# The first layer's values computed with tokens on partitions: x stationary, 512 weight columns moving

## The chip, the cores and the metric

The kernel runs on one core of a Trainium2 chip, as one launch. The metric is the device time of that launch in microseconds. Engines are named as in the profile: PE is TensorE, DVE VectorE, ACT ScalarE, POOL GpSimd, SP the queue that issues all DMAs.

## What is computed

One inference step of a two-layer trunk on 320 tokens: 256 of a prompt and 8 x 8 of a sample. The width is 1024. Layer 0 mixes tokens by chunked spatial gating, layer 1 by an mLSTM; each is followed by a gated feed-forward part. The change touches layer 0 alone:

```python
h = rmsnorm(x, norm_mix_g)                # 320 x 1024
u, v = split(gelu(h @ w_in), 2)           # w_in: 1024 x 4096; u and v: 320 x 2048
v = (v - mean(v)) * rsqrt(var(v) + eps) * ln_g + ln_b    # over the 2048, per token
mixed = einsum('gts,bnsgd->bntgd', tril(w_s), chunks of v) + b_s
y = (u * mixed) @ w_out                   # 2048 x 1024
```

The sample's normalised v is an output too. All tensors are fp32 and the product has to keep more bits than one fp32r matmul keeps. So each operand is split into a high part (rounded to fp32r) and a low part (the rest), and a product is three matmuls: high x high, high x low, low x high.

## The kernel before

x is held transposed: xT has 128 partitions (a slice of the width), 8 such slices k, and 320 columns (tokens). norm_block (L158 to L164) multiplies a slice by the norm's gain and splits it into xh (ACT, L163) and xl (DVE, L164). The token's own factor of the RMS norm, rc, is applied later, behind the matmuls: as a scale per partition where tokens lie on partitions, or as the row rb where they lie along columns. It needs the sum of squares (square_block), then norm_cols (three small matmuls, ms on DVE, a power on POOL at L196), and norm_row for rb.

Weights come from DRAM as blocks of 128 output columns: a tile "raw" of 128 x 8 x 128. weights() (L57) writes out the whole order of use as a list. prefetch(n, m) (L101) issues the DMAs of the first n entries on SP (L109) and splits the first m into wh (ACT copy, L124) and wl (DVE subtraction, L125). take() calls it with four loads and one split ahead. The pool "raw" has four buffers, wh and wl have three each. chunk and block run the matmuls: for each k, wh and then wl are stationary (128 x 128) and x moves, 320 columns at a time: wh x xh, wh x xl, wl x xh, into one PSUM bank of tag "pm". mm (L44) pins the matmuls to the order of the program; the other engines' orders are set by a scheduler that goes by the order of the code, free buffers and issue_after.

layer_a first computes v, weight blocks 16 to 31. Block b gives 128 values for 320 tokens, transposed to what is wanted. So DVE copies it to SBUF (vT, L289), v_nat turns it with three PE transposes (L50) into PSUM tiles pvt with tokens on partitions, and after each fourth block ACT applies gelu with scale rc (L269) and DVE takes the statistics (L270). Between the blocks stand the squares (after block 1), norm_cols and load_ws (the masks and mixing matrices, after block 3), norm_row (after block 5) and row_sums (after block 10). The third token tile holds the last 128 tokens, of which the lower 64 partitions repeat prompt tokens. Then come the 16 blocks of u, the normalisation of v (v_stats, normalise), the mixing (mix), and the output product. PSUM has three banks of tag "pm" and five of tag "pa".

run() starts with ten warm-up matmuls on a tile of ones (pw), loads the first 16 columns of vecs (8 KB), and then four times: two slices of x in one DMA (320 KB), a weight piece, the split of both slices. The first weight block is cut in pieces of 2, 2 and 4 slices, the second in 4 and 4.

Of the kernel before, what the change touches and what calls it, by code (L numbers as in the profile page):

```python
# [22 lines left out]
KD = D // P  # L23
DA = 2048
KA = DA // P
NH = 8
# [11 lines left out]
class Net:  # L38
# [19 lines left out]
    def weights(self):  # L58

        I = self.I  # L60
        q = []

        def add(w, b, *groups, k0=0):
            for kn in groups:
                q.append((w, b, k0, kn))
                k0 += kn

        add(I["a_win"], 16, 2, 2, 4)
        add(I["a_win"], 17, 4, 4)
        for b in [*range(18, 32), *range(16)]:  # L70
            add(I["a_win"], b, 8)
        for b in range(KD):
            add(I["a_wo"], b, 8, 8)

        def ffn(l):
            for b in range(2 * KF):
                add(I["f_up"][l], b, 8)
            for b in range(KD):
                add(I["f_dn"][l], b, 8, 7, 7)

        ffn(0)
# [21 lines left out]
    def prefetch(self, n, m):  # L103

        nc = self.nc
        while len(self.loaded) < min(n, len(self.wq)):
            w, b, k0, kn = self.wq[len(self.loaded)]
            raw = self.wraw.tile([P, 8, P], F32, tag="raw", name="raw")
            nc.sync.dma_start(raw[:, :kn, :], w[b, :, k0:k0 + kn, :])  # L109
            self.loaded.append(raw)  # L110
        while len(self.halved) < min(m, len(self.wq)):
            i = len(self.halved)
            raw, kn = self.loaded[i], self.wq[i][3]
            self.loaded[i] = None
# [9 lines left out]
            self.last_split = nc.scalar.copy(wh[:, :kn, :], raw[:, :kn, :])  # L124
            nc.vector.tensor_tensor(wl[:, :kn, :], raw[:, :kn, :], wh[:, :kn, :].bitcast(F32), op=SUB)  # L125
            self.halved.append((wh, wl))

# [16 lines left out]
    def block(self, kt, rhs):  # L144

        ps = self.psm.tile([P, 512], F32, tag="pm", name="pm")
        done = 0
        while done < kt:
            kn = self.wq[self.used][3]
            self.chunk(ps, lambda k: rhs(done + k), done == 0, done + kn == kt)  # L150
            done += kn
        return ps


    def vec(self, c):
# [26 lines left out]
    def norm_cols(self, parts=None, twice=False):  # L182

        nc = self.nc
        parts = parts or [self.acc]
        pc = self.psa.tile([P, 512], F32, tag="pa", name="pc")
        pv = pc[:, 0:6].rearrange("p (t e) -> p t e", e=2)
        for t in range(3):
            for i, a in enumerate(parts):
                self.mm(pv[:, t, :], self.tokens(a, t), self.ones[:, :2], i == 0, i == len(parts) - 1)  # L190
        rc = self.tp.tile([P, 3], F32, tag="rc", name="rc", bufs=2)
        ms = self.tp.tile([P, 3], F32, tag="ms", name="ms", bufs=2)
        nc.vector.tensor_scalar(ms, pv[:, :, 0], 1.0 / D, EPS, op0=MULT, op1=ADD)
        if twice:
            nc.scalar.copy(ms[:64, 2:3], ms[64:, 2:3])
        nc.gpsimd.tensor_tensor(rc, ms, self.mhalf.to_broadcast([P, 3]), op=ALU.pow)  # L196
        self.rc = rc

    def norm_row(self):
# [28 lines left out]
    def layer_a(self):  # L228
        nc, tc, I, O = self.nc, self.tc, self.I, self.O
        with tc.tile_pool(name="ya", bufs=1) as yp, tc.tile_pool(name="la", bufs=1) as lp:  # L230
# [11 lines left out]
            pvt = {}  # L242

            def load_ws():
                nc.sync.dma_start(ws, I["a_ws"])
                nc.sync.dma_start(trit, I["trit"])
                nc.gpsimd.memset(wss[:64], 0.0)
# [3 lines left out]
                nc.gpsimd.tensor_tensor(ws, ws, trit.unsqueeze(1).to_broadcast([P, NH, P]), op=MULT)  # L251
                nc.gpsimd.tensor_tensor(wss[64:], wss[64:], bdt[64:].unsqueeze(1).to_broadcast([64, NH, 64]), op=MULT)

            def row_sums():
                for i in range(2):
# [1 line left out]
                    self.mm(pr, self.ones, ws[:, 4 * i:4 * i + 4, :], True, True)  # L257
                    nc.scalar.copy(rsum[:, 4 * i:4 * i + 4, :].rearrange("p g t -> p (g t)"), pr)

            def v_nat(b, vT):  # L260
                q, c = b // 4, b % 4
                if c == 0:
                    pvt[q] = [self.psa.tile([P, 512], F32, tag="pa", name="pvt") for _ in range(3)]
                for t in range(3):
                    self.tr(pvt[q][t][:, c * P:(c + 1) * P], self.tokens(vT, t), self.ident)
                if c == 3:
                    for t in range(3):
                        vv = v[:, t, q * 512:(q + 1) * 512]
                        nc.scalar.activation(vv, pvt[q][t], AF.Gelu_apprx_tanh, scale=self.rc[:, t:t + 1])  # L269
                        nc.vector.bn_stats(st[:, t, q, :], vv)  # L270

            prev = None
            for b in range(16):
                ps = self.block(KD, self.x_rhs)
                if b == 1:
                    with tc.issue_after(self.last_split.ins):
                        for m in range(KD):
                            self.square_block(m)
                if b == 3:
                    self.norm_cols()  # L280
                    load_ws()
                if b == 5:
                    self.norm_row()
                if b == 10:
                    row_sums()
                if prev is not None:
                    v_nat(b - 1, prev)
                prev = lp.tile([P, T], F32, tag="vT", name="vT", bufs=2)
                nc.vector.tensor_copy(prev, ps[:, :T])  # L289

            ve = lp.tile([P, 3], F32, name="ve_a")
            rs = lp.tile([P, 3], F32, name="rstd_a")

            def v_stats():
                for t in range(3):
                    nc.vector.bn_aggr(mv[:, t, :], st[:, t])
                nc.vector.tensor_scalar(ve, mv[:, :, 1], EPS, None, op0=ADD)
                nc.gpsimd.tensor_tensor(rs, ve, self.mhalf.to_broadcast([P, 3]), op=ALU.pow)
                nc.vector.scalar_tensor_tensor(ve, mv[:, :, 0], -1.0, rs, op0=MULT, op1=MULT)

            def normalise(q):
                for t in range(3):
                    vv = v[:, t, q * 512:(q + 1) * 512]
                    nc.scalar.activation(vv, vv, AF.Identity, scale=rs[:, t:t + 1], bias=ve[:, t:t + 1])

            def v_rows(q):
                cs = slice(q * 512, (q + 1) * 512)
# [30 lines left out]
            for b in range(16):  # L338
                ps = self.block(KD, self.x_rhs)
                if b == 0:  # L340
                    v_nat(15, prev)
# [582 lines left out]
    def run(self):  # L924
        nc, tc, I, O = self.nc, self.tc, self.I, self.O
        with tc.tile_pool(name="const", bufs=1) as cp, tc.tile_pool(name="xp", bufs=1) as xp, \
# [15 lines left out]
            nc.scalar.activation(warm, self.mhalf, AF.Gelu_apprx_tanh)  # L942
            nc.vector.memset(self.ones, 1.0)
            pw = psa.tile([P, 512], F32, tag="pa", name="pw")
            for i in range(10):
                self.mm(pw[:, :P], self.ones, self.ones, True, True)
            nc.sync.dma_start(self.vecs[:, :16], I["vecs"][:, :16])
            for i in range(4):
                nc.sync.dma_start(self.xT[:, 2 * i:2 * i + 2, :], I["xT"][:, 2 * i:2 * i + 2, :])
                self.prefetch(i + 1, 0)  # L950
                for m in (2 * i, 2 * i + 1):
                    self.norm_block(m, V_MIX)
                self.prefetch(i + 1, min(i + 1, 3))
            nc.sync.dma_start(self.ident, I["ident"])
            nc.sync.dma_start(self.vecs[:, 16:], I["vecs"][:, 16:])
            self.layer_a()
            self.ffn(0, V_MIX + 8)
            self.layer_b()
# [15 lines left out]
def _lay_out(i):  # L974
# [6 lines left out]
    a["a_win"] = _blocks(i["a_w_in"][0])  # L981
# [80 lines left out]
```

## Time and profile before

| | us |
|---|---|
| median of three runs | 983.28 (981.37 to 983.53) |
| the profiled execution, own time | 980.58 |
| its span, first to last instruction | 978.8 |
| PE busy | 965.3 |
| DVE busy | 700.0 |
| ACT busy | 511.4 |
| POOL busy | 95.7 |

The page of the profile gives busy time by engine, the chain of work that ended last, and the costliest groups of instructions. The trace behind it answers by window, in order of time, by tile and by shape. A matmul's record begins when it starts and overlaps the next, so the pace of a run of matmuls is read from the chain (time of a piece over its count), not from the mean of one. A plain fp32 matmul leaves two records. The granted clock was 0.997 over the span. A weight block's matmuls are named pm; pvt are the transposes of v, pc, pb and pr those of norm_cols, norm_row and row_sums.

### The profile page before, as it was taken

Reading aid. Unit: us, or ns where it says so; the run is one execution under the profiler, and the core shown is the slowest. Engines: PE = TensorE matmul, PEld = TensorE weight load, DVE = VectorE, ACT = ScalarE, POOL = GpSimd, SP = SyncE. Lnnn points to the kernel's source line nnn. Section 1 sums busy time; section 2 is a strip of 40 time slices with the busy share of each in tenths; the row PEclk is TensorE's granted clock in tenths of the full one; section 3 lists DMA queues with packets and bytes.
Section 4 is the critical chain, followed back from the end, with each engine's and each line's share of the span. In section 5 each row is a group of like instructions: output and inputs, shape, how many; then the busy total and the mean of one; then the engine's idle time right before and its main releaser. Section 6 shows DMA issues by size and latency. Waiting matters only on the chain.

```text
span 978.8 us, 17589 instructions
## 1 busy us (share of the span) xinstructions
PE 965.3 (99%) x6695; PEld 958.9 (98%) x6695; DVE 700.0 (72%) x1358; ACT 511.4 (52%) x918; POOL 95.7 (10%) x268
## 2 busy tenths in 40 slices
PE   8999999999999999999999999999999999999996
PEld 8999999999999999999999999999999999999996
DVE  6647985577777764559999988787787777775442
ACT  6437444455544543349676766565655455544332
POOL 0100000010000000013231111111101000000000
PEclk9999999999999999999999999999999999999998
DMA  8535334444444454554464654544354444444541
GB/s 280 201 130 157 128 136 149 151 150 152 151 142 156 141 158 141 155 172 166 170 210 169 205 192 163 175 168 143 127 204 148 151 151 151 152 146 148 145 131 54
DMA packets 55591, 154.63 MB, mean 158 GB/s; under 512 B 6563, under 2 KB 17443, under 8 KB 55507
## 3 DMA queue, kind: packets, MB, share of 16 engines
q1 hardware_dynamic: 55506, 153.51, 47.1%
q8 instruction: 53, 0.87, 0.4%
q14 instruction: 32, 0.25, 0.1%
HBM read 141.55 MB, written 11.94 MB: 157 GB/s over the span
## 4 chain that ended last, share of the span: by engine, by line
PE 82%; issue 10%; DVE 4%; ACT 2%; DMA 1%; SPq 0%; POOL 0%; DVEq 0%; POOLq 0%; ACTq 0%
PE pm L47 74%; PE num L47 2%; PE pcs L47 1%; PE pmix L47 1%; DVE wl L125 1%; DMA C<-in_C 1%; DVE bcv L599 1%; PE pvt L50 1%; ACT wh L124 0%; PE pv L50 0%; PE psc L47 0%; PE pCp L47 0%; DMA xT<-in_xT 0%; PE phn L50 0%; PE pg L47 0%
## 5 line engine op out<-in xcount | busy, mean ns | idle before, releaser
L124 ACT CAST wh<-raw 128x1024 fp32r<-128x1024 f32 (+3 forms) x253 | 257.7, 1019 | 354.4 <-PE pm L47 196.8
L47 PE MATMUL pm<-xh,wh 128*128 128x320 f32 x1344 | 419.3, 312 | 1.4 <-ACT wh L124 1.4
L47 PE MATMUL pm<-xh,wl 128*128 128x320 f32 x1344 | 415.9, 309 | 2.1 <-DVE wl L125 1.9
L47 PE MATMUL pm<-xl,wh 128*128 128x320 f32 x1344 | 415.1, 309 | 0.0
L125 DVE TENSOR_TENSOR wl<-raw,wh 128x1024 fp32r<-128x1024 f32 (+3 forms) x253 | 299.6, 1185 | 117.9 <-ACT wh L124 115.2
L47 PEld LDWEIGHTS pm<-xh,wl 128*128 128x128 f32 x1344 | 252.3, 188 | 3.4 <-DVE wl L125 3.4
L47 PEld LDWEIGHTS pm<-xh,wh 128*128 128x128 f32 x1344 | 252.5, 188 | 2.4 <-ACT wh L124 2.1
L47 PEld LDWEIGHTS pm<-xl,wh 128*128 128x128 f32 x1344 | 252.5, 188 | 0.2
L47 PE MATMUL pm<-yh_f,wh 128*128 128x320 f32 x352 | 109.0, 310 | 0.0
L47 PE MATMUL pm<-yl_f,wh 128*128 128x320 f32 x352 | 108.5, 308 | 0.0
L47 PE MATMUL pm<-yh_f,wl 128*128 128x320 f32 x352 | 108.5, 308 | 0.0
L47 PEld LDWEIGHTS pm<-yl_f,wh 128*128 128x128 f32 x352 | 66.1, 188 | 0.0
L47 PEld LDWEIGHTS pm<-yh_f,wh 128*128 128x128 f32 x352 | 66.1, 188 | 0.0
L47 PEld LDWEIGHTS pm<-yh_f,wl 128*128 128x128 f32 x352 | 66.1, 188 | 0.0
L393 DVE SCALAR_TENSOR_TENSOR fcv<-fpad,vecs,fcv 128x336 f32<-128x336 f32 x88 | 49.6, 566 | 2.2 <-ACT fcv L391 0.7
L216 DVE TENSOR_TENSOR xT<-pm,xT 128x320 f32<-128x320 f32 x40 | 19.5, 490 | 41.9 <-PE pm L47 41.9
L47 PE MATMUL pm<-ylb,wh 128*128 128x320 f32 x128 | 39.9, 312 | 0.5 <-DVE ylb L813 0.4
L47 PE MATMUL pm<-yhb,wh 128*128 128x320 f32 x128 | 40.0, 312 | 0.4 <-ACT yhb L812 0.4
L47 PE MATMUL pm<-yhb,wl 128*128 128x320 f32 x128 | 39.6, 309 | 0.0
L47 PE MATMUL pm<-yh_a,wh 128*128 128x320 f32 x128 | 39.6, 309 | 0.0
L47 PE MATMUL pm<-yh_a,wl 128*128 128x320 f32 x128 | 39.5, 308 | 0.0
L47 PE MATMUL pm<-yl_a,wh 128*128 128x320 f32 x128 | 39.5, 308 | 0.0
(254 smaller groups left out, 1261.0 us busy)
## 6 DMA issues: line engine op xcount, KB each, us to landing
raw<-in_f_up SPq DMA_DIRECT2D x88, 512.0 KB, 3.2
raw<-in_b_win SPq DMA_DIRECT2D x48, 512.0 KB, 3.4
raw<-in_a_win SPq DMA_DIRECT2D x30, 512.0 KB, 3.3
raw<-in_f_dn SPq DMA_DIRECT2D x32, 448.0 KB, 3.2
C<-in_C SPq DMA_DIRECT2D x32, 258.0 KB, 3.7
raw<-in_a_wo SPq DMA_DIRECT2D x16, 512.0 KB, 3.7
raw<-in_f_dn SPq DMA_DIRECT2D x16, 512.0 KB, 3.5
out_Cs<-C SPq DMA_DIRECT2D x32, 256.0 KB, 2.7
```

Of the source, the lines that this page charges most:

```text
L47: self.pin(self.nc.tensor.matmul(out, lhsT, rhs, start=start, stop=stop))
L50: self.pin(self.nc.tensor.transpose(out, in_, ident))
L124: self.last_split = nc.scalar.copy(wh[:, :kn, :], raw[:, :kn, :])
L125: nc.vector.tensor_tensor(wl[:, :kn, :], raw[:, :kn, :], wh[:, :kn, :].bitcast(F32), op=SUB)
L216: self.nc.vector.tensor_tensor(x, ps[:, :T], x, op=ADD)
L393: nc.vector.scalar_tensor_tensor(cv, pd[:, i:i + NC], self.vec(w + i * KF), cv, op0=MULT, op1=ADD)
L599: nc.vector.scalar_tensor_tensor(cv, pd[:, i:i + NC], self.vec(w + 16 * i), cv, op0=MULT, op1=ADD)
```

## The change

In the v half the operands change places. The weights of v are laid out anew as a_wv: four groups of 512 columns, and in a tile two slices k of 512 columns each. `natural` keeps x stationary and moves 512 weight columns:

```python
def natural(self, ps, xs, hooks):
    k = 0
    while k < KD:
        for f in hooks.get(k, ()):
            f()
        (wh, wl), kn = self.take()
        for j in range(0, kn, 4):
            w, u = [x[:, j:j + 4, :].rearrange("p a b -> p (a b)") for x in (wh, wl)]
            h0, h1 = self.xh[:, k, :P], self.xh[:, k, P:TP]
            l0, l1 = self.xl[:, k, :P], self.xl[:, k, P:TP]
            a, z = k == 0, k == KD - 1
            for t, x, y, st, sp in ((0, h0, w, a, False), (1, h1, w, a, False), (0, l0, w, False, False),
                                    (1, l1, w, False, False), (2, xs[:, k, :], w, a, False), (0, h0, u, False, z),
                                    (1, h1, u, False, z), (2, xs[:, k, :], u, False, z)):
                self.mm(ps[t], x, y, st, sp)
            k += 1
```

Each group fills three whole PSUM banks: two for the prompt's two tiles and one for the sample. xs holds in its columns 0 to 63 the sample's xh and in 64 to 127 its xl, both copied by POOL; so the third bank holds the two parts' products on separate halves of the partitions, and they are added afterwards. (That also adds xl x wl, which was left out before.) Groups 0 and 2 use the banks of tag "pm", 1 and 3 those of "pa".

```diff
-        add(I["a_win"], 16, 2, 2, 4)
-        add(I["a_win"], 17, 4, 4)
-        for b in [*range(18, 32), *range(16)]:
+        for b in range(4):
+            add(I["a_wv"], b, 4, 4)
+        for b in range(4, 16):
+            add(I["a_wv"], b, 8)
+        for b in range(16):
             add(I["a_win"], b, 8)
...
-            self.last_split = nc.scalar.copy(wh[:, :kn, :], raw[:, :kn, :])
+            if i:
+                self.last_split = nc.scalar.copy(wh[:, :kn, :], raw[:, :kn, :])
+            else:
+                nc.vector.tensor_copy(wh[:, :kn, :], raw[:, :kn, :])
...
+            def x_parts(k):
+                self.norm_block(k, V_MIX)
+                nc.gpsimd.tensor_copy(xs[:, k, :64], self.xh[:, k, TP:T])
+                nc.gpsimd.tensor_copy(xs[:, k, 64:], self.xl[:, k, TP:T])
+
+            for k in range(4):
+                x_in(k)
+                if k:
+                    self.prefetch(k + 1, 0)
+            x_parts(0)
+            nc.sync.dma_start(self.ident, I["ident"])
+            nc.sync.dma_start(self.vecs[:, 16:], I["vecs"][:, 16:])
+            nc.gpsimd.memset(mv, 0.0)
+            nc.gpsimd.memset(v[:64, 2, :], 0.0)
...
+                with tc.issue_after(self.rc_made.ins):
+                    nc.gpsimd.tensor_tensor(ws, ws, trit.unsqueeze(1).to_broadcast([P, NH, P]), op=MULT)
+                    nc.gpsimd.tensor_tensor(wss[64:], wss[64:], bdt[64:].unsqueeze(1).to_broadcast([64, NH, 64]), op=MULT)
...
-            def v_nat(b, vT):
...
-                ps = self.block(KD, self.x_rhs)
...
+            def group(q, hooks):
+                pool, tag = (self.psa, "pa") if q % 2 else (self.psm, "pm")
+                vps[q] = [pool.tile([P, 512], F32, tag=tag, name="pv_a") for _ in range(3)]
+                self.natural(vps[q], xs, hooks)
+
+            def v_out(q):
+                cs = slice(q * 512, (q + 1) * 512)
+                ps = vps.pop(q)
+                tmp = lp.tile([P, 512], F32, tag="vs", name="vs_a", bufs=2)
+                nc.scalar.copy(tmp[64:], ps[2][:64])
+                nc.vector.tensor_tensor(tmp[64:], ps[2][64:], tmp[64:], op=ADD)
+                for t, src, r in ((0, ps[0], slice(0, P)), (1, ps[1], slice(0, P)), (2, tmp, slice(64, P))):
+                    vv = v[r, t, cs]
+                    nc.scalar.activation(vv, src[r], AF.Gelu_apprx_tanh, scale=self.rc[r, t:t + 1])
+                    nc.vector.bn_stats(st[r, t, q, :], vv)
...
+            group(0, {k: (lambda k=k: rows_in(k),) for k in range(KD)})
+            group(1, {0: (squares,), 6: (self.norm_cols, lambda: v_out(0))})
+            group(2, {0: (lambda: v_out(1), load_ws), 4: (self.norm_row,)})
+            group(3, {0: (lambda: v_out(2),), 4: (row_sums,)})
+            v_out(3)
...
-            for i in range(10):
+            self.prefetch(1, 0)
+            for i in range(7):
                 self.mm(pw[:, :P], self.ones, self.ones, True, True)
-            nc.sync.dma_start(self.vecs[:, :16], I["vecs"][:, :16])
-            for i in range(4):
-                nc.sync.dma_start(self.xT[:, 2 * i:2 * i + 2, :], I["xT"][:, 2 * i:2 * i + 2, :])
-                self.prefetch(i + 1, 0)
-                for m in (2 * i, 2 * i + 1):
-                    self.norm_block(m, V_MIX)
-                self.prefetch(i + 1, min(i + 1, 3))
```

The slices of x now come one by one (160 KB each): SP issues weight piece 0, vecs, x row 0, x row 1, weight piece 1, x row 2, weight piece 2, and so on. Group 0 takes weight pieces of one slice k (256 KB); the other groups take two slices (512 KB). Its hook rows_in(k) loads slice k + 4 of x and splits slice k + 1. The wh copy of piece 0 moves from ACT to DVE. In the built program the order on PE is that of `natural`; on POOL the power for rc stands ahead of the two mask products; SP places the loads of the masks in group 2. Vectors over v's third tile (statistics, gelu, normalisation) work on its upper 64 partitions, and its lower half is zeroed. The u half and all that follows keep their instructions.

More of the change, by code (lines that the diff above doesn't have):

```diff
@@ L152, in block @@
         return ps
+    def natural(self, ps, xs, hooks):
[3 more added lines that the diff above has]
+                f()
+            (wh, wl), kn = self.take()
+            for j in range(0, kn, 4):
[8 more added lines that the diff above has]
+                k += 1
     def vec(self, c):
@@ L195, in norm_cols @@
             nc.scalar.copy(ms[:64, 2:3], ms[64:, 2:3])
-        nc.gpsimd.tensor_tensor(rc, ms, self.mhalf.to_broadcast([P, 3]), op=ALU.pow)
+        self.rc_made = nc.gpsimd.tensor_tensor(rc, ms, self.mhalf.to_broadcast([P, 3]), op=ALU.pow)
         self.rc = rc
@@ L241, in layer_a, with x_in @@
             bdt = lp.tile([P, 64], F32, name="bdt")
-            pvt = {}
+            xs = lp.tile([P, KD, P], F32R, name="xs_a")
+            nc.sync.dma_start(self.vecs[:, :16], I["vecs"][:, :16])
+            def x_in(k):
+                nc.sync.dma_start(self.xT[:, k, :], I["xT"][:, k, :])
+            def x_parts(k):
[11 more added lines that the diff above has]
+            nc.gpsimd.memset(v[:64, 2, :], 0.0)
             def load_ws():
@@ L250, in load_ws @@
                 nc.sync.dma_start(bs, I["a_bs"].to_broadcast([P, NH, P]))
-                nc.gpsimd.tensor_tensor(ws, ws, trit.unsqueeze(1).to_broadcast([P, NH, P]), op=MULT)
-                nc.gpsimd.tensor_tensor(wss[64:], wss[64:], bdt[64:].unsqueeze(1).to_broadcast([64, NH, 64]), op=MULT)
+                with tc.issue_after(self.rc_made.ins):
+                    nc.gpsimd.tensor_tensor(ws, ws, trit.unsqueeze(1).to_broadcast([P, NH, P]), op=MULT)
+                    nc.gpsimd.tensor_tensor(wss[64:], wss[64:], bdt[64:].unsqueeze(1).to_broadcast([64, NH, 64]), op=MULT)
             def row_sums():
@@ L258, in row_sums @@
                     nc.scalar.copy(rsum[:, 4 * i:4 * i + 4, :].rearrange("p g t -> p (g t)"), pr)
-            def v_nat(b, vT):
[L261 to L270, printed above, removed]
@@ L272, in layer_a @@
-            prev = None
-            for b in range(16):
-                ps = self.block(KD, self.x_rhs)
[L275 to L289, printed above, removed]
+            def group(q, hooks):
+                pool, tag = (self.psa, "pa") if q % 2 else (self.psm, "pm")
+                vps[q] = [pool.tile([P, 512], F32, tag=tag, name="pv_a") for _ in range(3)]
+                self.natural(vps[q], xs, hooks)
@@ new lines, in squares, with rows_in @@
+            def squares():
+                with tc.issue_after(self.last_split.ins):
+                    for m in range(KD):
+                        self.square_block(m)
+            def rows_in(k):
+                if k + 4 < KD:
+                    x_in(k + 4)
+                if k + 1 < KD:
+                    x_parts(k + 1)
+            vps = {}
+            group(0, {k: (lambda k=k: rows_in(k),) for k in range(KD)})
+            group(1, {0: (squares,), 6: (self.norm_cols, lambda: v_out(0))})
@@ L295, in v_stats @@
                 for t in range(3):
-                    nc.vector.bn_aggr(mv[:, t, :], st[:, t])
+                    r = slice(64 * (t // 2), P)
+                    nc.vector.bn_aggr(mv[r, t, :], st[r, t])
                 nc.vector.tensor_scalar(ve, mv[:, :, 1], EPS, None, op0=ADD)
@@ L302, in normalise @@
                 for t in range(3):
-                    vv = v[:, t, q * 512:(q + 1) * 512]
-                    nc.scalar.activation(vv, vv, AF.Identity, scale=rs[:, t:t + 1], bias=ve[:, t:t + 1])
+                    r = slice(64 * (t // 2), P)
+                    vv = v[r, t, q * 512:(q + 1) * 512]
+                    nc.scalar.activation(vv, vv, AF.Identity, scale=rs[r, t:t + 1], bias=ve[r, t:t + 1])
             def v_rows(q):
@@ L340, in layer_a @@
                 if b == 0:
-                    v_nat(15, prev)
                     v_stats()
@@ L944, in run @@
             pw = psa.tile([P, 512], F32, tag="pa", name="pw")
-            for i in range(10):
+            self.prefetch(1, 0)
+            for i in range(7):
                 self.mm(pw[:, :P], self.ones, self.ones, True, True)
-            nc.sync.dma_start(self.vecs[:, :16], I["vecs"][:, :16])
-            for i in range(4):
-                nc.sync.dma_start(self.xT[:, 2 * i:2 * i + 2, :], I["xT"][:, 2 * i:2 * i + 2, :])
-                self.prefetch(i + 1, 0)
-                for m in (2 * i, 2 * i + 1):
-                    self.norm_block(m, V_MIX)
-                self.prefetch(i + 1, min(i + 1, 3))
-            nc.sync.dma_start(self.ident, I["ident"])
-            nc.sync.dma_start(self.vecs[:, 16:], I["vecs"][:, 16:])
             self.layer_a()
@@ L980, in _lay_out @@
                                "f_conv_w", "b_conv_w")], axis=1))
-    a["a_win"] = _blocks(i["a_w_in"][0])
+    w = _blocks(i["a_w_in"][0])
+    a["a_win"] = np.ascontiguousarray(w[:16])
+    a["a_wv"] = np.ascontiguousarray(w[16:].reshape(4, 4, P, 4, 2, P).transpose(0, 3, 2, 4, 1, 5).reshape(16, P, 8, P))
     a["a_wo"] = _blocks(i["a_w_out"][0])
```

## The prediction

> **What bounds the kernel now.** I read the page first (busy shares, then the chain that ended last), then the chain in order of time for the first 215 us, then the windows by stage.
>
> ```profile
> span 978.8 us, 17589 instructions
> PE 965.3 (99%) x6695; PEld 958.9 (98%) x6695; DVE 700.0 (72%) x1358; ACT 511.4 (52%) x918; POOL 95.7 (10%) x268
> PE 82%; issue 10%; DVE 4%; ACT 2%; DMA 1%; SPq 0%; POOL 0%; DVEq 0%; POOLq 0%; ACTq 0%
> ```
>
> ```profile
> 0.00:10.00 10.00, 7.25 (x34) 5.75 (x34) 4.45 (x12) 6.27 (x13) 0.72 (x5) 1.00 0.78 251
> 37.00:61.00 24.00, 24.00 (x162) 22.95 (x162) 12.15 (x17) 8.64 (x11) 0.00 (x0) 1.00 0.42 144
> ```
>
> The second fence holds two rows of the windows: PE, PEld, DVE, ACT and POOL busy time, the granted clock, the DMA share and GB/s. TensorE is the bound: only the first 10 us hold idle PE time (7.25 busy). In the steady part of the v half (37 to 61 us) DVE is busy 12.15 of 24 us and ACT 8.64, so whatever the change takes from or gives to them there is hidden behind PE. So the change is worth what it does to PE's own column time, plus what it does to the start.
>
> ```profile
> 2.19 4.31 DMA xT<-in_xT
> ...
> 10.13 5.25 PE pm L47 x34
> 15.39 0.33 PE pvt L50 x3
> 15.71 3.52 PE pm L47 x24
> ...
> 75.98 0.33 PE pvt L50 x3
> ...
> 139.83 59.91 PE pm L47 x408
> ```
>
> Up to 10.13 us the chain is xT's transfer and the splitting of x and of the weights; from there PE never lets go. Two blocks (48 matmuls) end at 15.39, and 34 of them lie in 10.13 to 15.39, so 14 were done before, worth 14 x 0.147 = 2.05 us. PE thus stands as if it had begun without a gap at 10.13 - 2.05 = **8.08 us**. That is the effective start to compare.
>
> **Part 1, PE's column time.** Removed: 16 blocks of 24 matmuls with 320 moving columns (3.52 us each) and the 48 transposes (0.33 us per three): 16 x 3.85 = 61.6 us. Added: 4 groups x 8 k x 8 matmuls = 256 matmuls with 512 moving columns. The sample's xh and xl share one stationary tile, so wh and wl each pass over it once; columns per k and group go from 4 x 3 x 320 = 3840 to 8 x 512 = 4096, 7% more, in 8 matmuls where there were 12. No fp32r matmul with 512 columns is in the trace, so its price is bounded from its neighbours in the chain, later in the run (pcs, pMb) and in this stage (pb, pr):
>
> ```profile
> 31.39 0.54 PE pb L47 x2
> ...
> 51.18 1.72 PE pr L47 x4
> ...
> 478.69 0.48 PE pcs L47 x4
> 479.16 0.18 PE pMb L47
> ```
>
> And rows of the groups by shape, which give the widths (partitions x columns):
>
> ```profile
> L47 PE MATMUL pcs<-vh,kgz 128*128 128x256 f32 x64 | 17.7, 301 | 0.0
> L47 PE MATMUL pMb<-X,sel 128*128 128x392 f32 x8 | 2.8, 353 | 0.0
> L47 PE MATMUL pb<-dg,ones 128*128 128x320 f32 x8 | 2.8, 432 | 0.0
> L47 PE MATMUL pr<-ws_a,ones 128*128 128x512 f32 x4 | 1.9, 591 | 0.0
> ```
>
> By the chain, 256 columns take 0.48/4 = 0.120 us, 320 take 59.91/408 = 0.1468, 392 take 0.18 (one, rounded). Per column that is 0.469, 0.459 and 0.459 ns: nearly proportional. At 0.459 ns, 512 columns take **0.235 us**; that is what I take, being the nearest row's rate and the one with 408 samples. The line through 256 and 320 (0.42 ns for each further column) gives 0.1468 + 192 x 0.00042 = 0.227, the low end from fp32r rows; 0.469 ns a column gives 0.240, the high end. Sum: 256 x 0.235 = 60.1 us, a gain of 61.6 - 60.1 = **1.5 us** (3.5 at 0.227, 0.2 at 0.240).
>
> pb and pr are plain fp32, and each of their records costs 0.27 us at 320 columns and 0.43 at 512: 0.84 ns a column, which I read as two passes of 0.42. If the new matmuls ran at one such pass, they would take 0.215 us; that is a rival below. The Trainium skill, "TensorE: Matmul & The Clock Gate", section "Wait — 56ns, not 53.3ns?", says that warm matmuls follow each other at N / 2.4 GHz plus about 2.5 ns, which is 215.7 ns at 512 columns. By that, 320 columns would take 136 ns; the row above has 147, so here the trace does not agree for fp32r.
>
> **Part 2, the start.** Before, SP sends vecs, then two rows of x (320 KB), then a weight piece, alternating. After, it sends the first weight piece (256 KB), vecs, x row 0 (160 KB), x row 1, weight piece 1, x row 2, and so on. The first matmul now needs piece 0 and x row 0 (424 KB with vecs), then one piece and one row per k, and each k is 8 x 0.235 = 1.88 us of PE work.
>
> ```profile
> 0.81 0.39 SPq L947 DMA_DIRECT2D vecs<-in_vecs  x1
> 1.25 0.42 SPq L949 DMA_DIRECT2D xT<-in_xT  x1
> ...
> 4.14 1.02 ACT L163 ACTIVATE xh<-xT,vecs 128x320 fp32r<-128x320 f32 x2 [1.83 <-DMA xT<-in_xT]
> ...
> 7.45 0.39 ACT L124 CAST wh<-raw 128x256 fp32r<-128x256 f32 x1
> ```
>
> The rows above are in order of time (start, duration, instruction); those below are groups by shape (count, busy, mean ns of one):
>
> ```profile
> L163 ACT ACTIVATE xh<-xT,vecs 128x320 fp32r<-128x320 f32 x32 | 17.5, 560 | 3.2 <-DMA xT<-in_xT 2.9 <-DVE xT L216 0.2
> L164 DVE SCALAR_TENSOR_TENSOR xl<-xT,vecs,xh 128x320 fp32r<-128x320 f32 x32 | 17.1, 546 | 4.7 <-ACT xh L163 4.7
> L124 ACT CAST wh<-raw 128x512 fp32r<-128x512 f32 x3 | 1.8, 613 | 0.5 <-DMA raw<-in_a_win 0.5
> L125 DVE TENSOR_TENSOR wl<-raw,wh 128x512 fp32r<-128x512 f32 x3 | 2.1, 686 | 0.0
> L590 POOL COPY bpad<-bst 128x24 f32<-128x24 f32 x16 | 6.3, 404 | 38.4 <-DVE bcv L599 31.7 <-DVE mv L746 5.2 <-DMA bst<-in_b_state 1.3
> L635 POOL TENSOR_SCALAR_AFFINE_SELECT w<-w 128x128 f32<-128x128 f32 x16 | 4.3, 293 | 20.4 <-ACT w L633 20.4
> ```
>
> 328 KB had landed at 4.14 us, 776 KB at 2.19 + 4.31 = 6.50, 904 KB by 7.45 at the latest. On that line 424 KB land at 4.65; the new order sends its first large piece one issue (0.44 us) earlier, so I take 4.5 (bounds 4.1 and 5.0). DVE meanwhile makes wh and wl of piece 0 (a copy no dearer than the 0.69 of the subtraction, then 0.69), which ends near 5.0 if the piece is there by 3.6. xh takes 0.56, so PE begins at 5.1; xl is there at 5.65, where two matmuls end at 5.57; the sample's tile follows by a POOL copy, which 24 and 128 columns bracket at 0.3 to 0.4 us: 6.05, where the fourth matmul ends at 6.12. The row stalls about 0.1 and k = 0 ends at 7.1. Piece 1 (840 KB in all) lands near 6.6 and is cast by 7.25: PE waits some 0.15. After that the feed runs ahead (by the same line piece 2, 1256 KB, is cast before 9, where it is wanted at 9.1; ACT has 0.56 + 0.61 and DVE 0.55 + 0.69 us a k against 1.88). Effective start: 7.25 - 1.88 = **5.4 us**, a gain of **2.7 us**. Bounds: 4.7 with everything early (gain 3.4), 6.6 with x at 5.0 and piece 1 half a microsecond late (gain 1.5).
>
> The raw ring has four buffers, so piece i + 4 goes out when piece i is split, at PE's start of k = i - 2 plus 1.3 us; with a landing of 4.3 us and a cast of 0.61 it is there 6.2 us later, and it is wanted six k, 11.3 us, later. That holds up to a landing of 9 us.
>
> SP's queue: the first eleven issues are eleven as before, 0.4 us each; x rows 4 to 7 follow behind ident and vecs, each one k ahead of its piece, and row 4 is wanted at 5.4 + 4 x 1.88 = 12.9.
>
> The clock at the start is the soft spot. The warm-up matmuls fall from ten to seven. Of the tile pw, in the windows 1 to 3.9 and 4 to 5 us (ns minimum/median/maximum, first and last start):
>
> ```profile
> L47 PE MATMUL pw<-ones x13: 371/421/582, 1.2 to 3.9; 128*128 128x128 f32 x13
> ```
>
> ```profile
> L47 PE MATMUL pw<-ones x9: 274/275/421, 3.7 to 4.8; 128*128 128x128 f32 x9
> ```
>
> Thirteen records start between 1.2 and 3.9 us, 2.7/12 = 0.22 us apart and 421 ns long; then they are 275 ns long and at most 1.1/8 = 0.14 apart: PE is slow at first, although the page calls the clock 1.00 throughout. Seven matmuls are 14 records and end near 4.2, just past that change; the real ones follow at 5.1. I take the change as made by then, as before; if PE were still at half its rate, k = 0 would cost up to another 1.9 us, which I keep as a bound. The Trainium skill, same page, section "What's actually happening", gives half rate until about 3.4 us of activity, in a window that does not start with the kernel. The rows agree with such a change 2.7 us after the first matmul; by that rule a window that ends later would leave k = 0 slow.
>
> **Part 3, what is hidden.** Gone from DVE: 16 copies of vT, and the wait of the transposes on them. New: four ACT copies and DVE additions of 64x512, sixteen POOL copies in the start, a memset of v's empty 64x2048 on POOL, four times the row below, done by 3.5 us, before xh exists. ACT's gelu and DVE's statistics keep their count and shape. None comes near PE in the row for 37 to 61 us; cover gone, one such step would cost its 0.5 to 0.7 us. One new dependence can bite: group 2 reuses the three banks of group 0, which wait for the row norm, made only in group 1 at k = 6, 2 x 1.88 = 3.75 us ahead.
>
> ```profile
> L247 POOL MEMSET wss_a<- 64x512 f32 x1 | 0.5, 517 | 0.3 <-POOLq L1044 0.3
> ws_a<-in_a_ws SPq DMA_DIRECT2D x1, 512.0 KB, 7.4
> L196 POOL TENSOR_TENSOR rc<-ms,mhalf 128x3 f32<-128x3 f32 x4 | 3.4, 854 | 54.8 <-DVE ms L193 54.4 <-ACT ms L195 0.4
> L269 ACT ACTIVATE v_a<-pvt,rc 128x512 f32<-128x512 f32 x12 | 7.4, 682 | 0.0
> ```
>
> After norm_cols' matmuls: about 0.2 for ms, 0.85 for the power on POOL, then two gelus of 0.68 on ACT (a 1.05 us weight cast queued ahead of them runs beside the power): 2.4 of 3.75 us, slack 1.4. Queued behind the waiting gelu on ACT is the cast for group 2's third chunk, 7.5 us ahead of its need. load_ws's transfers, 7.4 us to landing, go out in group 2 and are wanted in group 3 at k = 4, over 15 us later. In the built order POOL's power now stands ahead of the two mask products on POOL, which wait for trit. Cost: nothing. From the u half on, order and work are the same.
>
> **Sum.** -1.5 - 2.7 = -4.2 us on the profiled execution: 980.58 (span 978.8 and 1.8 around it) to 976.4. That execution lies 2.7 below the median of the three runs, 983.28 (981.37 to 983.53), so for the median I forecast 983.28 - 4.2 = **979.1 us**. About 0.2%, 2 us, is what a measurement of this kernel can tell from no change.
>
> **Rivals.**
> - *One pass at 0.42 ns a column* (0.215 us a matmul): 55.0 us in place of 60.1, the sum becomes -9.3: 974.0. For it: pr at 512 columns. Against it: every fp32r row, 0.459 or more. The skill's spacing above gives nearly the same. Chance 0.08.
> - *The start gives nothing*: x row 0 and piece 1 land late, or PE is cold through k = 0, so that the effective start is near 8 again; what is left is -1.5: 981.8. For it: transfers share the rings (776 KB took until 6.50), and PE now needs both operands at k = 0. Against it: half as much x is needed first. Chance 0.13.
> - *The stationary load shows* (the slower side): every new matmul loads another x tile, and part of that load stands outside the stream. Three transposes take 0.33 us, 0.11 each for 128 columns, where 0.459 ns a column would be 0.059: 0.05 us of load shows. If all 0.05 showed in each of the 256, that costs 12.8 us: 991.9. It decides from 4.2/256 = 16 ns a matmul. Against it: the 320-column matmuls also load each time and show nothing, and 512 columns hide more. Chance 0.05.
> - *The bank wait in group 2* beyond its slack would cost what exceeds 1.4 us, inside the range; it has no chance of its own.
>
> **How the numbers follow.** Forecast 0.74, rivals 0.08, 0.13 and 0.05. The forecast's own bounds: price 0.227 and early start, -3.5 - 3.4: 976.4; price 0.240 and late start, -0.2 - 1.5: 981.6. The range goes a little beyond both for the spread of the runs before (2.2 us), 975.4 to 982.0, and takes in most of the start rival; 0.08 below and 0.05 above stay outside, with some of the forecast's tails. Faster by over 0.2% (under 981.3): the forecast but 0.03 and the first rival, and a little of the second: 0.81. Within 0.2%: 0.13. Slower: 0.06.
>
> **What would show it.** Between group starts 64 matmuls should take 15.0 us (14.5 at 0.227, 13.8 at 0.215). The first 512-column matmul should start near 5.1 and k = 1 near 7.2. Group 2's first matmul should follow group 1's last without a gap. Wrong would be: 421 ns-like spacing after 5 us, PE waiting on raw beyond k = 2, or a spacing of 250 ns.

## The result, and the profile after

| | before | after |
|---|---|---|
| median of six runs, us | 981.06 (980.09 to 983.53) | 976.48 (975.58 to 977.85) |
| ratio | | 0.9946, 95% interval 0.9933 to 0.9959 |
| profiled execution, us | 980.58 | 975.58 |
| its span, us | 978.8 | 973.9 |

The changed kernel is faster, by 4.6 us in the medians and by 4.0 to 6.6 us (0.41 to 0.67%) by the interval. The forecast was 4.2 less, at 979.1 in a range of 975.4 to 982.0. The absolute time lies 2.6 below 979.1 mostly because the three runs that the forecast started from had a median of 983.28 and the six have 981.06.

The page of the changed kernel:

```profile
span 973.9 us, 17241 instructions
PE 961.7 (99%) x6513; PEld 944.8 (97%) x6513; DVE 697.6 (72%) x1348; ACT 514.5 (53%) x922; POOL 103.2 (11%) x286
```

PE is busy 3.6 us less, in 182 records fewer; the bound is the same. The chain in order of time (start, duration, piece) shows where the time went. pv_a are the new 512-column matmuls:

```profile
1.72 2.93 DMA xT<-in_xT
...
4.74 0.57 ACT xh L186
...
5.36 26.64 PE pv_a L47 x112
31.99 0.57 PE pc L47 x6
32.56 11.24 PE pv_a L47 x48
43.80 0.54 PE pb L47 x2
44.34 14.85 PE pv_a L47 x64
59.19 1.72 PE pr L47 x4
60.90 7.42 PE pv_a L47 x32
68.32 17.60 PE pm L47 x120
...
135.35 59.91 PE pm L47 x408
```

The last row is the output product of layer 0. It started at 139.83 before and starts at 135.35 now: **4.48 us** of the gain stand already there. Every experiment below has the same row (pm x408, 59.91 us), so its start is used as the mark of each: it is read to hundredths, where the time of a run scatters by a microsecond and more. It is the mark of one execution, though, and the pace at which that execution began is in it: a second profile of the changed kernel, below, has it at 136.48.

Up to this mark the gain has the two parts of the forecast. A group of 64 matmuls takes 14.85 us, 0.232 each. The 104 from k = 1 to norm_cols take 31.99 - 7.60 = 24.39, 0.2345 each (7.60 is in the next fence). So 256 cost between 59.4 and 60.0 us, against 61.6 for the blocks and transposes: about 2 us. And k = 1 starts at 7.60, which is 8 x 0.2345 = 1.88 after an effective start of 5.72, against 8.08 before: 2.4 us. Together 4.4.

The first microseconds of the changed kernel, in order of time:

```profile
5.34 1.07 DVE L187 SCALAR_TENSOR_TENSOR xl<-xT,vecs,xh 128x320 fp32r<-128x320 f32 x2 [0.64 <-ACT xh L186]
...
5.36 0.73 PE L47 MATMUL pv_a<-wh,xh 128*128 128x512 f32 x2 [0.85 <-ACT xh L186]
5.37 0.24 POOL L275 CAST xs_a<-xh 128x64 fp32r<-128x64 f32 x1 [2.27 <-ACT xh L186]
...
5.82 0.24 POOL L275 CAST xs_a<-xh 128x64 fp32r<-128x64 f32 x1 [0.22 <-ACT xh L186]
...
6.01 0.70 POOL L276 CAST xs_a<-xl 128x64 fp32r<-128x64 f32 x2
6.16 0.62 ACT L127 CAST wh<-raw 128x512 fp32r<-128x512 f32 x1 [0.40 <-DMA raw<-in_a_wv]
...
6.57 0.49 PE L47 MATMUL pv_a<-wh,xs_a 128*128 128x512 f32 x1
...
7.60 0.62 PE L47 MATMUL pv_a<-wh,xh 128*128 128x512 f32 x2
```

k = 0 lasts 2.24 us in place of 1.88. It waits for xl (its products start at 6.00, where two matmuls of 0.235 would have ended at 5.83), then for the sample's tile. POOL does the copy of xh for k = 1 (5.82) ahead of the copy of xl for k = 0 (6.01): the scheduler put it there. Weight piece 1 is cast by 6.78 and holds nobody up.

### The profile page after: what moved, and what is told of

Read it like the earlier page. It is cut to its first block, busy times and chain, and to the rows that moved or that the text cites. A ratio compares the mean times of both kernels' runs of the same rounds, so it can differ in the third digit from the quotient of the medians.

```text
span 973.9 us, 17241 instructions
## 1 busy us (share of the span) xinstructions
PE 961.7 (99%) x6513; PEld 944.8 (97%) x6513; DVE 697.6 (72%) x1348; ACT 514.5 (53%) x922; POOL 103.2 (11%) x286
## 4 chain that ended last, share of the span: by engine, by line
PE 82%; issue 10%; DVE 5%; ACT 2%; DMA 0%; POOL 0%; SPq 0%; DVEq 0%; POOLq 0%; ACTq 0%
PE pm L47 69%; PE pv_a L47 6%; PE num L47 2%; PE pcs L47 1%; PE pmix L47 1%; DVE wl L130 1%; DVE bcv L648 1%; DVE Cl L758 1%; PE pv L50 0%; ACT wh L127 0%; PE psc L47 0%; PE pCp L47 0%; PE phn L50 0%; DMA xT<-in_xT 0%; PE pg L47 0%
## 5 line engine op out<-in xcount | busy, mean ns | idle before, releaser
L127 ACT CAST wh<-raw 128x1024 fp32r<-128x1024 f32 (+2 forms) x253 | 257.0, 1016 | 341.4 <-PE pm L47 164.1
L130 DVE TENSOR_TENSOR wl<-raw,wh 128x1024 fp32r<-128x1024 f32 (+2 forms) x254 | 299.9, 1181 | 131.8 <-ACT wh L127 128.8
L47 PE MATMUL pm<-xh,wh 128*128 128x320 f32 x1216 | 378.1, 311 | 0.0
L47 PE MATMUL pm<-xh,wl 128*128 128x320 f32 x1216 | 376.0, 309 | 1.1 <-DVE wl L130 1.1
L47 PE MATMUL pm<-xl,wh 128*128 128x320 f32 x1216 | 375.6, 309 | 0.0
L47 PEld LDWEIGHTS pm<-xh,wl 128*128 128x128 f32 x1216 | 228.3, 188 | 1.6 <-DVE wl L130 1.6
L47 PEld LDWEIGHTS pm<-xh,wh 128*128 128x128 f32 x1216 | 228.4, 188 | 0.3
L47 PEld LDWEIGHTS pm<-xl,wh 128*128 128x128 f32 x1216 | 228.4, 188 | 0.3
```

Source lines behind the costliest of these rows:

```text
L47: self.pin(self.nc.tensor.matmul(out, lhsT, rhs, start=start, stop=stop))
```

## The experiments

**Is the price of the form its columns?** Two kernels ask it from both sides. The first cuts every matmul in two:

```diff
-                    self.mm(ps[t], x, y, st, sp)
+                    for c in (0, 256):
+                        self.mm(ps[t][:, c:c + 256], x, y[:, c:c + 256], st and c == 0, sp and c == 256)
```

> The changed kernel with every 512-column matmul cut into two of 256: 512 matmuls, the same columns. Theory (price nearly proportional to columns, 0.0023 us + 0.452 ns a column through 320 and 512): a pair costs 0.236 instead of 0.2335, the v half 0.6 us more, up to 1.6 by the 0.120 us that 256 columns took before; first pmix at 86.5 to 87.5. Rival (a fixed cost of 13 ns or more in each matmul, so that the gain is the smaller count): 3.4 us more, 89.3.

Its chain:

```profile
6.73 0.24 POOL xs_a L276
6.96 0.45 POOL xs_a L277
...
7.46 25.82 PE pv_a L47 x216
...
45.84 15.14 PE pv_a L47 x128
...
137.30 59.91 PE pm L47 x408
```

15.14 us for 128 halves in place of 14.85 for 64 wholes: 0.2366 a pair, 2% more, or 1.2 us over the 256. That is 4.5 ns for each matmul more, so the rival's fixed cost of 13 ns falls. The mark comes 1.95 us later, above what was expected, and the top of the chain says why: the sample's copies on POOL. x row 1 landed at 6.08 here, its copy of xh stood on POOL ahead of the copy of xl for k = 0, and the first matmul on the sample's tile began at 7.46 in place of 6.57. The same order on POOL as above, with a later row, costs 0.9 us.

The second kernel undoes the packing of the sample:

```diff
-  (2, xs[:, k, :], w, a, False), ... (2, xs[:, k, :], u, False, z)
+  (2, h2, w, a, False), (2, l2, w, False, False), ... (2, h2, u, False, z)
+  # h2, l2 = self.xh[:, k, T - P:T], self.xl[:, k, T - P:T]; xs, its copies and the addition gone
```

> The changed kernel without the packing: the sample's xh and xl stay separate stationary tiles (128 tokens each), nine matmuls per k and group in place of eight, no copies into xs, no addition behind the group. Theory (PE's columns are the price): 32 x 0.232 = 7.4 us more on PE, first pmix near 93.3, the whole run 7 us slower than the changed kernel and 2 to 3 us slower than before. Rival (the gain lies in the start and in the form, packing is a detail hidden beside PE): within 1 us of the changed kernel.

983.46 us (981.36 to 983.81, ten runs) against 981.02: ratio 1.0014, interval 1.0001 to 1.0027, so a little slower than before. Its chain:

```profile
49.45 16.36 PE pv_a L47 x72
...
142.75 59.91 PE pm L47 x408
```

Nine matmuls a k cost 16.36 us a group against 14.85, and the mark is 7.40 later. That this is the 7.4 that was expected is partly luck: the price of one fell to 0.227 (16.36/72), so the nine cost 5.5 to 6 us more over the four groups, and this profiled execution began at half pace (below), which adds about 1.2. By time the sign is told only just (1.0001 at the lower end), but without those 1.2 the mark would still lie 1.7 behind that of before. So the packing of the sample's two parts into one stationary tile decides the sign. In PE's time the new form wins 2 us with eight matmuls per k and loses about 4 with nine (288 x 0.227 = 65.4 against 61.6), more than the start gives back.

**Do the transposes pay?** The kernel before, with each transpose of v issued twice:

```diff
-                    self.tr(pvt[q][t][:, c * P:(c + 1) * P], self.tokens(vT, t), self.ident)
+                    for _ in range(2):
+                        self.tr(pvt[q][t][:, c * P:(c + 1) * P], self.tokens(vT, t), self.ident)
```

> The kernel before with each of the 48 transposes of v issued twice. Theory (the transposes lie wholly on PE's path and their removal pays for the added columns): 16 x 0.33 = 5.3 us more, first pmix near 95.7, 0.5% slower than before. Rival (they fill gaps that PE would have anyway, and the gain of the change is in the matmuls): under 1 us.

986.61 us (985.82 to 988.04): ratio 1.0053, interval 1.0037 to 1.0070, 5.6 us in the medians. Its chain:

```profile
16.31 0.66 PE pvt L50 x6
16.96 3.52 PE pm L47 x24
...
146.04 59.91 PE pm L47 x408
```

0.66 us where 0.33 stood, sixteen times: 5.3 us, all of it on the path. The mark is 6.2 later; the other 0.9 stands already ahead of the first transposes (16.31 in place of 15.39) and is this execution's start: the granted clock was 0.50 from 8.25 to 11.66, where PE began only 12 matmuls. The matmuls themselves became dearer by the change (16 x 3.52 = 56.3 to nearly 60 us), so the gain in PE's time is the transposes and nothing else.

**Where does the start gain come from?** The old form with the new feed: piece 0 first, rows one by one, first split on DVE, with seven warm-up matmuls and, later, with ten.

```diff
+            self.prefetch(1, 0)
-            for i in range(10):
+            for i in range(7):
...
-                nc.sync.dma_start(self.xT[:, 2 * i:2 * i + 2, :], I["xT"][:, 2 * i:2 * i + 2, :])
+                for m in (2 * i, 2 * i + 1):
+                    nc.sync.dma_start(self.xT[:, m, :], I["xT"][:, m, :])
```

> The old form (weights stationary, transposes) with the new feed: weight piece 0 first, x in single rows, first split on VectorE, seven warm-up matmuls. Theory (the start gain comes from the new form's need: it wants one row of x per 1.88 us, where a block of the old form wants all eight rows within 3.5 us): the effective start stays near the last row's landing, 7.5 to 8.1 us against 8.08 before, and the first mixing matmul (pmix, 90.40 us before, 85.92 after) starts at 89.8 to 90.4. Rival (the order of the transfers alone makes the start gain): 88.0.

> The old form with the new feed and ten warm-ups, to take the clock out of the first look at it. Theory (the old form wants all eight rows of x within 3.5 us, so single rows bring it little): output product at 139.0 to 140.0 against 139.83. Rival (the order of transfers makes the start gain by itself): 137.5.

The chain with seven (first fence) and with ten:

```profile
5.05 4.02 DMA raw<-in_a_win
...
9.76 7.13 PE pm L47 x36
...
141.36 59.91 PE pm L47 x408
```

```profile
5.51 5.68 DMA xT<-in_xT
...
12.42 6.05 PE pm L47 x29
...
142.94 59.91 PE pm L47 x408
```

The marks are 1.5 and 3.1 us later than before's, where 137.5 was the rival's; both lie outside what was expected. Both executions ran part of this stretch at half pace: 36 matmuls in 7.13 us in place of 5.3, 29 in 6.05 in place of 4.3. Without that an estimated 139.5 and 141.2 are left, the first within its expectation, the second still worse. In neither does the feed by itself bring the old form anything. With seven, PE waited last for a weight piece that was issued behind six single rows of x, at 5.05, and landed at 9.07; with ten, for the seventh row of x, issued at 5.51 and landed at 11.2. Why that row took 5.7 us there and 4.0 in the run with seven, no run shows. The start gain belongs to the new form, which wants a row every 1.88 us.

The changed kernel with x in pairs of rows:

```diff
-                nc.sync.dma_start(self.xT[:, k, :], I["xT"][:, k, :])
+                if k % 2 == 0:
+                    nc.sync.dma_start(self.xT[:, k:k + 2, :], I["xT"][:, k:k + 2, :])
```

> The changed kernel with x in pairs of rows, 320 KB each. Theory (the first matmul waits for the x that is sent first): it starts 0.5 to 0.8 us later than the 5.36 us of the changed kernel, the second k follows, and the first pmix starts at 86.4 to 86.8. Rival (size of x's transfers doesn't matter, the weights' does): 85.9.

Chain, then two rows of the windows (PE busy, granted clock, DMA share, GB/s):

```profile
1.72 3.95 DMA xT<-in_xT
...
6.37 27.98 PE pv_a L47 x112
...
137.69 59.91 PE pm L47 x408
```

```profile
6.50:8.00 1.50, 1.50 (x5) 0.80 0.99 339
8.00:9.50 1.50, 1.50 (x5) 0.50 1.07 400
```

The pair lands at 5.67 in place of 4.65 and PE starts 1.01 us later, a little more than expected. The mark is 2.34 later. The windows show the rest: the clock fell to 0.50 between 7.4 and 10.8, after PE had stood still for 2.1 us behind the warm-up, in place of 0.85.

The last on the feed sends x row 0 ahead of weight piece 0 and puts wl's products ahead of xl's in each k:

```diff
-  (0, h0, w), (1, h1, w), (0, l0, w), (1, l1, w), (2, xs, w), (0, h0, u), (1, h1, u), (2, xs, u)
+  (0, h0, w), (1, h1, w), (0, h0, u), (1, h1, u), (0, l0, w), (1, l1, w), (2, xs, w), (2, xs, u)
-            self.prefetch(1, 0)          # ahead of x; now right behind row 0
```

> The changed kernel with vecs and x row 0 sent ahead of weight piece 0, and in each k the products of xh with both weight parts ahead of those with xl and the sample's tile. Theory (the first matmul waits for x row 0, then for xl and the sample's copy): first 512-column matmul at 4.5 to 4.8 us in place of 5.36, no wait for xl, second k at 6.8 to 7.1 in place of 7.60, first pmix at 85.1 to 85.4. Rival (the second k is held by weight piece 1, whatever stands first): 85.8 to 85.9. The time moves by under 0.1% either way.

977.47 us (975.41 to 977.64): ratio 0.9952, interval 0.9934 to 0.9970. The mark is at 137.40. A miss on both sides. In order of time:

```profile
4.84 0.56 ACT L186 ACTIVATE xh<-xT,vecs 128x320 fp32r<-128x320 f32 x1 [2.54 <-DMA xT<-in_xT]
5.44 0.61 DVE L187 SCALAR_TENSOR_TENSOR xl<-xT,vecs,xh 128x320 fp32r<-128x320 f32 x1 [4.34 <-ACT xh L186]
...
5.97 0.41 DVE L129 CAST wh<-raw 128x512 fp32r<-128x512 f32 x1
...
6.53 0.76 PE L47 MATMUL pv_a<-wh,xh 128*128 128x512 f32 x1 [2.02 <-DVE wh L129]
```

Sent second in place of third, row 0 landed no earlier (4.75). Weight piece 0, issued at 1.72 in place of 0.81, was 3.7 us under way and landed at 5.44 in place of 3.5, so wh could no longer be made while x was under way. And the scheduler put xl ahead of wh on DVE, which began wh at 5.97. PE so started 1.17 us later; the rest of the 2.05 is pace: the first nine matmuls of this execution lie about 0.43 us apart, up to 10.4 us.

**The clock at the start.** One warm-up matmul in place of seven:

```diff
-            for i in range(7):
+            for i in range(1):
                 self.mm(pw[:, :P], self.ones, self.ones, True, True)
```

> The changed kernel with one warm-up matmul in place of seven. Theory (PE runs at half its pace until it has been busy for some 2.7 us): the first 512-column matmuls follow each other at about 0.43 us instead of 0.23, for one to two k, and the first pmix starts 1.3 to 2.5 us later, at 87.2 to 88.4. Rival (the slow records of the warm-up are only those of plain fp32 or of the first instructions; the start is set by transfers): 85.9.

The mark is at 136.69, 1.34 later, as expected: the first nine 512-column matmuls lie about 0.427 us apart, up to 9.3 us. The changed kernel itself, without an edit, profiled a second time beside its variants, shows the same with its seven:

> The changed kernel again, beside the two others on the same chip. Expected: median 976 to 977.5, runs in two heaps about 1.6 us apart, by whether PE starts at full or at half pace.

Its pv_a rows in two windows by count (busy, clock, DMA), and its chain:

```profile
5.30:8.80 3.50, 3.49 (x8) 1.00 0.93 303
8.80:12.30 3.50, 3.50 (x16) 1.00 1.00 329
```

```profile
5.31 27.83 PE pv_a L47 x112
...
136.48 59.91 PE pm L47 x408
```

Eight matmuls in the first 3.5 us, sixteen in the next: half pace, while the clock column says 1.00 (it knows only changes that it recorded, and the first comes at 8.87). The mark is 1.13 later than in the first profile of the same kernel; part of the half pace hides in the waits of k = 0. The five runs spread from 975.55 to 977.64; the two heaps that were expected are not plain in so few. With ten warm-up matmuls again:

```diff
-            for i in range(7):
+            for i in range(10):
                 self.mm(pw[:, :P], self.ones, self.ones, True, True)
```

> The changed kernel with ten warm-up matmuls again, as before. Theory (the clock is decided in windows of 3.41 us whose place differs from run to run, and seven warm-ups fill too little of some of them, after which PE begins at half pace): PE is busy from 1.15 to about 5 us, a window that ends in it releases the clock, and the slow runs of the changed kernel go: output product (pm x408, 135.35 us in the changed kernel's profile, 139.83 before) at 135.2 to 136.2, median 0.3 to 1 us under the control. Rival (the number of warm-ups doesn't matter): the control's median and spread.

975.69 us (975.52 to 976.37, five runs) against the control's 976.63; ratio to before 0.9942, interval 0.9930 to 0.9955. The mark stands at 135.37, and the slower end of the spread is gone. Last, the same with wl's products ahead of xl's (the first two lines of the last diff on the feed), piece 0 staying first:

> As the last, and in each k the products of xh with both weight parts ahead of those with xl and the sample's tile. Theory (k = 0 loses 0.34 us to xl and 0.26 us to the sample's tile, and wl is there before them): output product 0.3 to 0.6 us before the last kernel's, in the same state of the clock. Rival (the second k is held by weight piece 1 anyway): the same place.

975.34 us (974.99 to 975.37): ratio 0.9936, interval 0.9924 to 0.9949, the best of all kernels here. Its chain:

```profile
1.15 4.64 PE pw L47 x20
5.79 25.88 PE pv_a L47 x112
...
43.92 14.71 PE pv_a L47 x64
...
134.75 59.91 PE pm L47 x408
```

The mark is 0.62 earlier, as expected; 0.36 of it had come by norm_cols, the rest is the pace (14.71 for 14.85). Both gains over the control are under 0.2%. The five runs of this last kernel all lie below the lowest of the kernel before it (975.52) and of the control (975.55). Ten warm-ups alone show in the spread: their mark, 135.37, is that of the changed kernel's first profile, which began at full pace by luck.

The other profiles say the same of the warm-up. Of the eight executions with seven warm-ups, four were at full pace by the first real matmul (the changed kernel, the halves, the pairs, the late norm below) and four were not (the control, nine a k, x first, the old form with seven). All five with ten (before, the transposes twice, the old form with ten, and the last two) were, by their second real matmul at the latest. Ten do not help against a later wait: in the transposes twice and in the old form with ten the clock fell to 0.50 for 3.4 us further on.

**The banks of group 2.** The norm's matmuls moved behind group 1:

```diff
-            group(1, {0: (squares,), 6: (self.norm_cols, lambda: v_out(0))})
+            group(1, {0: (squares,)})
+            self.norm_cols()
+            v_out(0)
```

> The changed kernel with the norm's three matmuls and the first group's outputs put behind group 1 instead of two k ahead of its end. Theory (group 2 takes group 0's banks, which wait for the chain ms 0.16, power 1.80, gelu 0.66 and 0.61): PE waits 2.7 to 3.2 us at group 2's first two matmuls, first pmix at 88.6 to 89.1. Rival (the scheduler or other banks cover it): 85.9.

The waits, the chain, and the windows by clock of that kernel:

```profile
PE pv_a L47 <- ACT v_a L318: 2.5, 1, 2.5
```

```profile
36.62 1.82 POOL rc L219
...
39.21 8.88 PE pv_a L47 x31
```

```profile
39.00:42.40 3.40, 3.19 (x8) 0.50 0.64 186
42.40:46.00 3.60, 3.60 (x17) 0.99 0.02 7
```

PE waits 2.5 us, as the theory has it, and then pays again: for the 3.4 us that follow the clock stands at 0.50, and 31 matmuls take 8.88 us in place of 7.3. The mark is at 139.61, 4.3 later, where 2.7 to 3.2 were expected. The Trainium skill, "TensorE: Matmul & The Clock Gate", section "What's actually happening", says that the clock is set by how busy the array was, in windows of 3413 ns that run freely. The 3.4 us at 0.50 agree with that.

## Why the prediction was right, step by step

- **PE's column time.** Forecast 0.235 us a matmul, measured 0.232 (a free group) to 0.2345 (in the start). Forecast gain 1.5, measured about 2.0. The nearly proportional price was the right reading of the rows for 256, 320 and 392 columns, and the nearest row's rate the right choice; cutting the matmuls in two agrees (0.118 for 256). By the spacing that the Trainium skill states ("TensorE: Matmul & The Clock Gate", section "Wait — 56ns, not 53.3ns?": 215.7 ns at 512 columns) it would have been 55 us; the measured 59.4 and more decide against it here.
- **The start.** Forecast 5.4, measured 5.72; gain 2.7 forecast, 2.4 measured. The mechanism was right: the old form gained nothing from the new feed. The steps within were not. Row 0 landed at 4.65 (4.5 forecast) and PE began at 5.36 (5.1). "The row stalls about 0.1" was 0.36: about half of it is the wait for xl, the other half the wait for the sample's tile, whose copy on POOL stood behind another; that order could have been read in the built program. "PE waits some 0.15" for piece 1 was nothing: it was cast at 6.78, not 7.25. The two errors nearly cancel. The feed also ran ahead by less than forecast: piece 2 was cast at 9.42, not before 9, just as k = 2 wanted it (9.47). And 8.08 is a little early: its 34 matmuls would take 4.99 us at 0.1468, their piece took 5.25, so counted back from the end of the second block (15.39 less 48 x 0.1468) the old start is 8.34. The new one, counted in the same way (31.99 less 112 x 0.232), is 6.01, a gain of 2.3.
- **The clock.** It was named as the soft spot with a bound of 1.9 us, and taken as released by 5.1. That held in the profiled execution and not in its repetition, where it cost 1.13. In the first it was luck: all 14 records of the warm-up are slow there too (421 ns and more), and full pace came only between the start of the last of them and the first real matmul. Seven warm-up matmuls leave it to chance, four times in eight; ten did not, in five profiles.
- **The banks.** Slack 1.4 us forecast. The power took 1.80 us in place of 0.85 (its nearest row, that of four, was the wrong one; L298's, 1.86, was nearer), and the second gelu was done at 35.94, where bank 1 was wanted near 36.5: 0.6 left. The wait cost nothing, as forecast. Had it come, it would have cost more than its length, as the late norm shows: 2.5 us of wait cost 4.1.
- **What was hidden** stayed hidden: in the changed kernel the trace lists no wait of PE from 9.5 us to the mark.
- **The sum.** 4.2 forecast, 4.48 at the mark, 4.9 in the span. The further 0.4 lies behind layer 0, where the change touches nothing; its cause is open. The piece of 176 matmuls in layer 1 stands at 705.89 in place of 711.06, so 0.7 are won there, and 0.2 are lost behind it.

Of the rivals, one pass at 0.42 ns a column is refuted by every group; the start that gives nothing did not come, though its half (a slow clock) did in some runs; the stationary load shows next to nothing, since twice the loads and matmuls, in the halves, cost 4.5 ns for each one more, where the rival had 50. The 0.05 us that the prediction read off the transposes need not be load: at the 0.84 ns a column of pb and pr, 128 columns take 0.108 us by themselves.

## What to carry to other kernels

Before turning a product's operands round, count its columns, price one matmul from rows of other widths, and set that against the transposes it saves; here a packing that removes one matmul in nine decides the sign. Look in the built order at what stands ahead of each small copy on the first step's path, on every engine. And keep PE busy without a gap until its first real matmul: here 2.1 us of idle time there (the pairs), or a single wait of 2.5 us later (the late norm), was followed by 3.4 us at half pace.

## What the runs showed of the hardware that was not expected

- A matmul in fp32r costs 0.118 us at 256 columns, 0.147 at 320, 0.232 at 512: 0.45 to 0.46 ns a column. At half pace 512 columns take 0.427 us, which is 1.84 times, not twice.
- The same 512 columns differ in price by 1 to 2% with the order and the tiles: 0.232 in the changed kernel, 0.230 with wl's products second, 0.227 with nine a k and no tile xs. No run here separates why.
- A wait on PE of 2.5 us cost 4.1: for the 3.4 us behind it the granted clock was 0.50.
- Sending 160 KB of x one place earlier in SP's queue did not make them land earlier (4.75 against 4.65 us).
